# A hybrid attention and delta-rule layer on one core: weights laid out by partition, the second half of x normed among the shift and scale's quarters, the values' turns one projection later

## The chip, the cores and the metric

The program runs on one core of a Trainium2 chip. The core has a matrix engine (TensorE, PE in the profile; its weight loads are PEld), VectorE (DVE), ScalarE (ACT), GpSimd (POOL) and SyncE (SP, which here only issues DMAs), and 16 DMA engines that move data between memory and the core. The metric is the device time of one execution in microseconds (us); the time of a kernel is the median of its runs.

## The reference, cut to what matters

The layer takes 1024 latent tokens and 256 context tokens of width 1024, modulates them by a shift and a scale that a small matrix product makes from a vector c (and c_ctx for the context), projects them with one matrix w_in of 4112 columns, and mixes them by neighbourhood attention and by a gated delta rule in both directions.

```
shift, scale, gate = jnp.split(jax.nn.silu(c) @ w_ada + b_ada, 3, axis=-1)
h = rmsnorm(x, g_pre) * (1.0 + scale[:, None]) + shift[:, None]
hc = rmsnorm(xc, g_pre) * (1.0 + scale_c) + shift_c
na_q, na_k, na_v, na_z, g_qkv, g_z, g_b, g_a = jnp.split(h @ w_in, IN_SPLITS, axis=-1)
...
o_na = neighborhood_attention(heads(na_q), heads(na_k), heads(na_v),
                              heads(na_kc), heads(na_vc), rpb)
q, k, v = gdn_qkv(g_qkv, conv_w)
...
o_g, o_gc = bidirectional_gdn(q, k, v, g, beta, qc, kc, vc, gc, betac)
y = jnp.concatenate([o_na * jax.nn.silu(na_z), o_g * jax.nn.silu(g_z)], axis=-1) @ w_out
x = x + gate[:, None] * rmsnorm(y, g_post)
```

## The kernel before

Matrix products run in 32-bit form as three products of high and low parts: every weight and every activation is split into hi (a copy in the matrix engine's own 32-bit type) and lo (the rest), and a product is hi·hi + lo·hi + hi·lo. So each group of products is three lines of the code: L446, L450, L451 where channels come out as partitions, and L459, L460, L461 where tokens do. The activations after the norm are the tiles hh and hl (128 partitions by 8 blocks of 128 channels by 1024 tokens), chh and chl for the context.

The first stage is `phase0`. It loads the first half of x (512 tokens, tiles x), turns it so that channels lie in the partitions (tile raw) and takes its sums of squares on ACT. A helper, `norms` (L216), makes a row of factors from such sums: an addition on DVE (L148), a power on POOL (L149), a spread on DVE (rr, L221), a turn on PE (prr, L224), a copy on ACT (rba for the first half, rbb for the second, L225). The shift and scale come in four quarters, each of 256 channels, by `ada(q)` (L266): four loads of w_ada into the tile wada (7 buffers), a matmul for each block of 128 rows into par (L276), a copy of par by DVE (rows, L288), four small matmuls that put the result into partitions (pa, L292), two short DVE operations (ab, am), and `modulate` (L235) for the quarter's two blocks of channels: a scaling on DVE (L238), the high part on ACT (L244), the low part on DVE or POOL (L245, L242). Then `products(q)` (L305) takes the two blocks into six sums that stay open over all quarters: values for four tiles of tokens (pv) and query and key (pq, pk).

Behind the quarters come the loads of a gate's weights (wg), the second half of x (tiles xta and xtb of 4 blocks by 256 tokens, `load_t`), its squares on ACT (xsa, xsb, L330) and their sums over channels by matmuls against a column of ones (pss, L335, one output column each), `norms`, the gate's projection (pz, L446 to L451 out of wgh and wgl), `mod(0)` and `mod(1)` for the second half, the second half's values and query and key, and the context (xtc).

The order on an engine is set by the code's order and by a scheduler that moves an instruction forward where its inputs are early. Loads of the first stage are chained on SP's queue by `chain` (L205), in the order of the code. A load waits for its buffer: x and the squares xs share a tag with 4 buffers, wada is shared by wg, xta and xtb.

`load_w` (L414) loads a piece of w_in, copies it on ACT into the high part and subtracts on POOL (L432) for the low part. In `phase2` the delta rule's inputs are projected, convolved (acc, L798 to L800, on DVE) and turned, head by head, by the steps of a string (L755): R the gate of the residual, V the values' convolution, p a projection of `projections`, T and B the turns of query and key, U the turns of the values (vtp on PE, L737; vs on ACT, L739, whose buffer is shared with the tile rot of T). Between the steps DVE solves small triangular systems (tb and vb, L989 and L992). One of the projections is that of the first 264 value channels (wl_nv, pv), whose weights are split in four pieces.

## Time and profile before

| | us |
|---|---|
| runs | 914.02, 919.75, 919.37 |
| median | 919.37 |
| the profiled execution | 925.77 |
| span of its core | 924.1 |
| PE busy | 865.4 (94%) |
| DVE busy | 534.1 (58%) |
| ACT busy | 418.3 (45%) |
| POOL busy | 371.2 (40%) |

The span is the time from the core's first to its last instruction in the profile. A row of a timeline reads: start, duration, engine, line of the code and operation, output and inputs, partitions by elements, count; in brackets how long the engine stood idle before it and what released it. A row of the table by stretches gives for each engine the busy time and the number of instructions, then the clock that was granted to PE (1.00 is full speed), the busy share of the DMA engines and the rate that they moved. A matmul of fp32 inputs stands in the trace as two rows, so that four matmuls of pa are 8 there, and 8 of pss are 16.

### The profile page before, as it was taken

What the parts mean: (1) busy time and instruction counts of PE and PEld (TensorE: products, weight loads), DVE (VectorE), ACT (ScalarE), POOL (GpSimd) and SP (SyncE); (2) the same over time, 40 slices, a digit from 0 to 9 for tenths busy, and PEclk for the clock granted to TensorE, in tenths of its full rate; (3) what the DMA queues carried; (4) which work ended last, traced back from release to release, by engine and by line L of the source; (5) the groups of instructions that cost most, each with busy time, mean ns of one, the idle gap of its engine ahead of it and who ended that gap; (6) DMA issues with size and microseconds to landing.
All of it is one profiled execution on the core that took longest, in us unless ns stands there. A gap on an engine that the chain in (4) does not pass through costs nothing.

```text
span 924.1 us, 16864 instructions
## 1 busy us (share of the span) xinstructions
PE 865.4 (94%) x6178; PEld 724.0 (78%) x6178; DVE 534.1 (58%) x1191; ACT 418.3 (45%) x1171; POOL 371.2 (40%) x435
## 2 busy tenths in 40 slices
PE   5998999999999998998997999899999997999997
PEld 3687988788788776778976878688888886788785
DVE  3416326535644699779437723477777775673442
ACT  4235323554654643651434534455556546553211
POOL 1313122263463461455231311566757558632110
PEclk9977999999999999999997999899999999799999
DMA  9853351254544723842899775999839324223261
GB/s 309 261 165 109 122 172 49 79 166 162 147 146 153 212 92 126 264 108 70 252 250 251 224 218 175 397 263 227 301 79 304 132 70 149 80 73 134 71 207 65
DMA packets 126441, 157.85 MB, mean 171 GB/s; under 512 B 29893, under 2 KB 99862, under 8 KB 124182
## 3 DMA queue, kind: packets, MB, share of 16 engines
q1 hardware_dynamic: 98870, 142.58, 49.8%
q10 hardware_dynamic: 27488, 14.19, 6.0%
q8 instruction: 49, 0.80, 0.4%
q14 instruction: 34, 0.28, 0.1%
HBM read 107.67 MB, written 52.42 MB: 173 GB/s over the span
## 4 chain that ended last, share of the span: by engine, by line
PE 69%; DMA 12%; DVE 12%; ACT 3%; issue 2%; SPq 1%; POOL 0%; ACTq 0%; DVEq 0%; POOLq 0%
PE py L1204 3%; PE py L1206 3%; PE py L1205 3%; PE pz L446 3%; PE pz L450 3%; PE pz L451 3%; PE pl L674 2%; PE pv L459 2%; PE po L701 2%; PE pv L460 2%; PE pl L683 2%; PE pv L461 2%; PE po L696 2%; DVE tb L989 2%; PE pc L670 2%
## 5 line engine op out<-in xcount | busy, mean ns | idle before, releaser
L662 POOL TENSOR_TENSOR gm<-gt,mk 128x288 f32<-128x288 f32 (+1 forms) x64 | 64.2, 1009 | 26.5 <-DVE nm L679 22.4
L1111 POOL TENSOR_SCALAR kd<-kt,kd 128x128 f32<-128x128 f32 x72 | 43.1, 603 | 35.7 <-PE pa L1130 35.1
L680 ACT ACTIVATE pt<-pt,nm 128x288 f32<-128x288 f32 (+1 forms) x64 | 36.8, 575 | 41.7 <-DVE nm L679 41.1
L446 PE MATMUL pz<-hh,wh_gz 128*128 128x512 f32 x112 | 46.3, 413 | 1.0 <-DVE sl_k L509 1.0
L450 PE MATMUL pz<-hl,wh_gz 128*128 128x512 f32 x112 | 45.7, 408 | 0.0
L451 PE MATMUL pz<-hh,wl_gz 128*128 128x512 f32 x112 | 45.3, 405 | 0.0
L678 DVE TENSOR_REDUCE mi<-pc 128x1 f32<-128x256 f32 x64 | 26.9, 421 | 30.1 <-PE pc L670 29.6
L460 PE MATMUL pv<-wh_nv,hl 128*128 128x264 f32 x128 | 39.7, 316 | 4.2 <-DVE hl L245 4.2
L459 PE MATMUL pv<-wh_nv,hh 128*128 128x264 f32 x128 | 38.3, 318 | 5.0 <-DVE st_z L534 3.6
L685 DVE COPY tl<-pl 96x384 f32<-96x384 f32 (+1 forms) x64 | 35.3, 552 | 11.0 <-PE pl L683 10.4
L679 DVE CUSTOM_DVE_ANT_0 pt<-pl,gm,mi 128x288 f32<-128x288 f32 (+1 forms) x64 | 36.0, 563 | 8.2 <-PE pl L674 4.6
L683 PE MATMUL pl<-c,pt 128*96 128x128 f32 (+1 forms) x192 | 34.3, 289 | 5.4 <-ACT pt L680 5.3
L461 PE MATMUL pv<-wl_nv,hh 128*128 128x264 f32 x128 | 39.0, 311 | 0.4 <-POOL wl_nv L432 0.4
L931 ACT ACTIVATE em<-em,gc 128x128 f32<-128x128 f32 x80 | 25.5, 390 | 30.5 <-DMA em<-gc_dram 26.0
L946 DVE SCALAR_TENSOR_TENSOR pm<-pk,beta,em 128x128 f32<-128x128 f32 x80 | 23.6, 344 | 24.6 <-PE pk L939 14.3
L989 DVE TENSOR_TENSOR tb<-ab,vb 120x31 f32<-120x31 f32 (+15 forms) x62 | 32.3, 521 | 7.7 <-DMA ab<-ab_dram 6.0
L950 POOL TENSOR_SCALAR_AFFINE_SELECT qe<-qe 128x256 f32<-128x256 f32 x32 | 26.9, 841 | 21.1 <-DVE qe L949 21.0
L460 PEld LDWEIGHTS pv<-wh_nv,hl 128*128 128x128 f32 x128 | 27.1, 213 | 8.8 <-DVE hl L245 4.5
L1114 POOL TENSOR_SCALAR vb<-v,beta 128x128 f32<-128x128 f32 x40 | 24.2, 605 | 24.1 <-DVE y L1120 16.3
L432 POOL TENSOR_TENSOR wl_gq<-wr_gq,wh_gq 128x512 fp32r<-128x512 f32 x8 | 15.1, 1899 | 44.8 <-ACT wh_gq L431 27.4
L459 PEld LDWEIGHTS pv<-wh_nv,hh 128*128 128x128 f32 x128 | 26.5, 216 | 8.1 <-DVE st_z L534 3.8
L1130 PE MATMUL pa<-vn,kd 128*128 128x128 f32 x144 | 28.8, 286 | 4.2 <-ACT vn L1128 3.1
(440 smaller groups left out, 2924.3 us busy)
## 6 DMA issues: line engine op xcount, KB each, us to landing
wada<-in_w_ada SPq DMA_DIRECT2D x32, 256.0 KB, 5.5
em<-gc_dram SPq DMA_DIRECT2D x20, 256.0 KB, 4.1
pm_dram<-pm SPq DMA_DIRECT2D x20, 256.0 KB, 2.8
pmf<-pm_dram SPq DMA_DIRECT2D x8, 640.0 KB, 7.2
tm_dram<-tm SPq DMA_DIRECT2D x8, 640.0 KB, 4.3
kk<-qk_dram SPq DMA_DIRECT2D x16, 320.0 KB, 8.6
tm<-tm_dram SPq DMA_DIRECT2D x4, 1280.0 KB, 9.7
kq_dram<-kq SPq DMA_DIRECT2D x4, 1152.0 KB
```

The source lines that it names most:

```text
L446: r = nc.tensor.matmul(ps, wh, xh, start=(k == 0), stop=False)
L450: nc.tensor.matmul(ps, wh, xl, start=False, stop=False)
L451: nc.tensor.matmul(ps, wl, xh, start=False, stop=(k == KC - 1))
L459: nc.tensor.matmul(ps, xh, wh, start=(k == 0), stop=False)
L460: nc.tensor.matmul(ps, xl, wh, start=False, stop=False)
L461: nc.tensor.matmul(ps, xh, wl, start=False, stop=(k == KC - 1))
L662: nc.gpsimd.tensor_tensor(gm[:, :n].rearrange("p (n c r) -> p n c r", c=nco, r=4), gv, mk[:, mo:mo + n].rearrange("p (n c r) -> p n c r", ...
L679: nc.vector.tensor_tensor_reduce(pt[:, :n], pl[:, :n], gm[:, :n], -1.0, mi, ALU.add, ALU.min, nm)
L680: nc.scalar.activation(pt[:, :n], pt[:, :n], AF.Exp, bias=nm, scale=-1.0, accum_out=sums[:, ct, hh, 0:1])
L683: nc.tensor.transpose(pl[:m, rc * P:(rc + 1) * P], pt[:, rc * m:(rc + 1) * m], self.ident)
L989: nc.vector.tensor_tensor(t3, bc(ab[:, 0:m, m:m + 1], [r, m, n]), bc(vb[:, m:m + 1, m:], [r, m, n]), ALU.mult)
L1111: nc.gpsimd.tensor_scalar(kd, kt_[:, t, :], self.kd[:, h, d, t:t + 1], None, ALU.mult)
```

## The change

It has four parts.

1. The host lays the weights out by partition. The shift and scale part of w_ada becomes an array of quarters in which a partition's rows follow each other, so one DMA brings a wada tile (4 KB a partition), where two brought it in pieces of 1 KB. The gate part becomes an array of its own. w_in becomes one flat array in which each piece that `load_w` loads lies in one run a partition (W_PARTS, W_OFF), so that the two-part pieces are one DMA too.
2. The second half of x is loaded behind the first quarter's weights, in four tiles of two blocks by 512 tokens (tag x). Its squares and their sums are taken with the second quarter, `norms` follows, and its blocks are modulated at a width of 512 among the third and fourth quarters. The squares, and rr of the norm, share the one buffer sq. The context's squares and sums are later, behind the products of the fourth quarter, and its modulation is ahead of the rest of the gate's projection.
3. In `load_w`, where the weights come in four pieces (halves=4), the subtract of the second and fourth piece runs on DVE.
4. In the string of steps the values' turns U stand behind the last projection p instead of ahead of it.

```diff
-        "xt": f("x").reshape(S, D)[512:].reshape(2, 256, 8, P).transpose(0, 3, 2, 1),
+        "xt": f("x").reshape(S, D)[512:].reshape(512, 8, P).transpose(2, 1, 0),
...
-                    for n in range(2):
-                        c0 = 1024 * n + 256 * q
-                        chain(wa[:, :, n, :], I["w_ada"][P * k2:P * k2 + 256, c0:c0 + 256].rearrange(
-                            "(k p) n -> p k n", p=P))
+                    chain(wa, I["w_ada"][q][:, k2:k2 + 2])
...
+            def load_t(src, nm, pool_tag, bufs, kk):
+                r = []
+                for k in range(0, KC, kk):
+                    w = p0.tile([P, kk, D // kk], F32, name=f"xt{nm}{k}", tag=pool_tag, bufs=bufs)
+                    chain(w, src[:, k:k + kk, :])
+                    r.extend(w[:, j, :] for j in range(kk))
+                return r
+
+            def squares(xr, nm, pss, kk):
+                n = D // kk
+                for k in range(0, KC, kk):
+                    s_ = p0.tile([P, kk, n], F32, name=f"xs{nm}{k}", tag="sq", bufs=1)
+                    for j in range(kk):
+                        nc.scalar.activation(s_[:, j, :], xr[k + j], AF.Square)
+                    for j in range(kk):
+                        for i in range(n // P):
+
+                            nc.tensor.matmul(pss[:, i:i + 1], s_[:, j, P * i:P * i + P], self.ones, start=(k + j + i == 0),
+                                             stop=(k + j == KC - 1 and i == n // P - 1))
+
+            def second(ks):
+                for k in ks:
+                    modulate(xr[k], self.hh[:, k, 512:], self.hl[:, k, 512:], k, 0, rb2)
+
+            ada(0)
+            xr = load_t(I["xt"], "a", "x", 4, 2)
+            ada(1)
+            products(0)
+            pss = at("pss", "tb", 2)
+            squares(xr, "a", pss, 2)
+            rb2 = rbt("b")
+            norms(g1, rb2, pss[:, 0:4], nc.vector)
+            ada(2)
+            products(1)
+            second(range(4))
+            ada(3)
...
+            xc = load_t(I["cxt"], "c", "wada", 7, 4)
+            products(2)
+            second((4, 5))
             products(3)
+            second((6, 7))
...
-            mod(0)
             next(gates)
...
+            src = self.I["w_in"]
+            (load or nc.scalar.dma_start)(raw.rearrange("p k n -> p (k n)"), bass.AP(
+                src.tensor, W_OFF[tuple(c0) if isinstance(c0, list) else ((c0, n),)] + k0 * n, [[KC * n, P], [1, kk * n]]))
             nc.scalar.copy(hi, raw)
-            nc.gpsimd.tensor_tensor(lo, raw, hi.bitcast(F32), ALU.subtract)
+            (nc.vector if halves > 2 and k0 % 4 else nc.gpsimd).tensor_tensor(lo, raw, hi.bitcast(F32), ALU.subtract)
...
-                for c in "RVppTpUpB":
+                for c in "RVppTppUB":
```

In the rows below a name ends in a number that tells buffers of the same kind apart, and the shape is that of one instruction. On PE, before, the fourth quarter's pa is followed by the third quarter's last products, the sums of squares of the second half stand behind these, and the fourth quarter's products behind the sums:

```order
L292 MATMUL pa_475<-c_60,rows_473 128x2 x4
L446 MATMUL pq_0_208<-hh,wqk_h 128x512
L450 MATMUL pq_0_208<-hl,wqk_h 128x512
L451 MATMUL pq_0_208<-hh,wqk_l 128x512
L446 MATMUL pq_0_208<-hh,wqk_h 128x512
L450 MATMUL pq_0_208<-hl,wqk_h 128x512
L451 MATMUL pq_0_208<-hh,wqk_l 128x512
L335 MATMUL pss<-ones,xsa_538 128x1 x4
L335 MATMUL pss<-ones,xsa_542 128x1 x4
```

On PE, now, behind the second quarter's products (the first two pieces of the squares, xsa_352 and xsa_363, were summed ahead of and among them):

```order
L467 MATMUL pk_0_209<-hl,wqk_h 128x512
L468 MATMUL pk_0_209<-hh,wqk_l 128x512
L347 MATMUL pss<-ones,xsa_374 128x1 x8
L347 MATMUL pss<-ones,xsa_385 128x1 x8
L242 MATMUL prr_402<-c_60,rr_400 128x128 x4
L291 MATMUL par_408<-wada_409,sc 32x512 x2
L291 MATMUL par_408<-wada_413,sc 32x512 x2
L291 MATMUL par_408<-wada_417,sc 32x512 x2
L291 MATMUL par_408<-wada_421,sc 32x512 x2
L307 MATMUL pa_437<-c_60,rows_435 128x2 x4
L291 MATMUL par_501<-wada_502,sc 32x512 x2
```

The norm of the second half (prr), the third quarter's par and its pa now follow the sums directly, with no products between them, and the fourth quarter's par stands in one piece.

On DVE, before, two quarters follow each other, each with its copy of rows, ab, am, two scalings and two low parts:

```order
L288 COPY rows_388<-par_355 128x512
L245 SCALAR_TENSOR_TENSOR hl<-raw,ab_310,hh 128x512 x2
L296 TENSOR_TENSOR ab_395<-pa_390,cols 128x8
L297 SCALAR_TENSOR_TENSOR am<-ab_395,cols 128x4
L238 SCALAR_TENSOR_TENSOR raw<-raw,am,rba 128x512 x2
L245 SCALAR_TENSOR_TENSOR hl<-raw,ab_395,hh 128x512 x2
L288 COPY rows_473<-par_440 128x512
```

On DVE, now, from the norm of the second half to the third quarter's low parts:

```order
L166 TENSOR_SCALAR rq_y_x_397<-pss 128x4
L239 TENSOR_SCALAR rr_400<-rq_y_x_397 128x512
L256 SCALAR_TENSOR_TENSOR xta_264<-xta_264,am,rbb 128x512 x2
L256 SCALAR_TENSOR_TENSOR xta_266<-xta_266,am,rbb 128x512 x2
L263 SCALAR_TENSOR_TENSOR hl<-xta_264,ab_255,hh 128x512
L263 SCALAR_TENSOR_TENSOR hl<-xta_266,ab_306,hh 128x512
L303 COPY rows_435<-par_408 128x512
L311 TENSOR_TENSOR ab_442<-pa_437,cols 128x8
L312 SCALAR_TENSOR_TENSOR am<-ab_442,cols 128x4
L256 SCALAR_TENSOR_TENSOR raw<-raw,am,rba 128x512 x2
L256 SCALAR_TENSOR_TENSOR xta_268<-xta_268,am,rbb 128x512 x2
L263 SCALAR_TENSOR_TENSOR hl<-raw,ab_442,hh 128x512 x2
```

Four scalings and two low parts of the second half stand ahead of the copy of the third quarter's rows, and two more scalings ahead of that quarter's own low parts.

On DVE in phase 2, before, behind the triangular solve's operations tb and vb, at the gate projection st_z that stands next to the first value channels' products:

```order
L989 TENSOR_TENSOR tb_3553<-ab_3550,vb_3552 120x207
L992 TENSOR_TENSOR vb_3552<-vb_3552,tb_3553 120x23x9
L989 TENSOR_TENSOR tb_3553<-ab_3550,vb_3552 120x220
L992 TENSOR_TENSOR vb_3552<-vb_3552,tb_3553 120x22x10
L534 SCALAR_TENSOR_TENSOR st_z_3866<-st_z_3866,pz_1_3841 128x512
```

and now:

```order
L449 TENSOR_TENSOR wl_nv_6_3854<-wr_nv_6_3852,wh_nv_6_3853 128x528
L1006 TENSOR_TENSOR tb_3511<-ab_3508,vb_3510 120x207
L551 SCALAR_TENSOR_TENSOR st_z_3824<-st_z_3824,pz_1_3799 128x512
L1009 TENSOR_TENSOR vb_3510<-vb_3510,tb_3511 120x23x9
L1006 TENSOR_TENSOR tb_3511<-ab_3508,vb_3510 120x220
```

The subtract of the fourth weight piece is on DVE, and st_z stands three operations of the solve earlier.

More of the change, by code (lines that the diff above doesn't have):

```diff
@@ L87, with by_partition @@
 MTOT = _o
+W_PARTS = ([((1288, 248), (4096, 16)), ((0, P), (512, P)), ((1024, 264),)]
+           + [((c, P),) for c in [1536] + [P * j + o for j in range(1, 4) for o in (0, 512, 1536)]
+              + [2048 + P * j for j in range(12)] + [3584 + P * j for j in range(4)]])
+W_OFF = {}
+_o = 0
+for _w in W_PARTS:
+    W_OFF[_w] = _o
+    _o += D * sum(_n for _, _n in _w)
+def by_partition(w):
+    return w.reshape(KC, P, -1).transpose(1, 0, 2)
 def layout_inputs(inp):
@@ L349, in phase0 @@
                 self.qk_out(0, i, 0, pqk[i])
-            def mod(j):
-                for k in range(KC):
-                    sl = slice(512 + 256 * j, 768 + 256 * j)
-                    modulate(xr[j][k], self.hh[:, k, sl], self.hl[:, k, sl], k, 0, rbs[j])
-            mod(0)
             next(gates)
             pss = at("pssc", "tb", 2)
-            xr.append(load_t(I["cxt"], "c", pss[:, 0:2]))
-            for j in range(2):
-                g = g1[2 * j:2 * j + 2]
-                if j == 0:
-                    mod(1)
-                    norms([0, 1], rbs[2], pss[:, 0:2], nc.vector)
-                self.values(vp, wv, 1, g)
+            squares(xc, "c", pss, 4)
+            rbc = rbt("c")[:, :256]
+            norms([0, 1], rbc, pss[:, 0:2], nc.vector)
+            self.values(vp, wv, 1, g1)
             for i in range(2):
@@ L394, in res_gate @@
             nc.sync.dma_start(wt.rearrange("p (k n) -> p k n", k=2),
[L395 removed]
+                              I["w_adg"][q][:, k:k + 2, :])
             wts.extend(wt[:, 256 * j:256 * j + 256] for j in range(2))
```

41 lines of the change are left out of this document (6 added, 35 removed).

## The prediction

> **What bounds the kernel now.** I read the table of engine times by stretch first, with the granted clock beside it, because the change touches one early stage and one place at 330 to 425 us.
>
> ```profile
> core 0: us, PE busy (x) PEld busy (x) DVE busy (x) ACT busy (x) POOL busy (x), PEclk, DMA share, GB/s
> 0.00:25.00 25.00, 15.72 (x73) 9.29 (x75) 8.74 (x16) 11.13 (x19) 4.37 (x11) 0.91 0.99 309
> ...
> 60.00:80.00 20.00, 20.00 (x86) 18.20 (x86) 3.88 (x12) 4.26 (x10) 1.02 (x1) 0.63 0.26 80
> 80.00:95.00 15.00, 10.75 (x66) 10.26 (x64) 12.54 (x23) 10.19 (x26) 6.93 (x8) 0.77 0.41 125
> 130.00:230.00 100.00, 100.00 (x524) 83.55 (x523) 50.87 (x75) 45.10 (x109) 35.60 (x45) 1.00 0.39 120
> 230.00:330.00 100.00, 100.00 (x521) 81.45 (x520) 59.44 (x90) 54.94 (x136) 44.21 (x44) 1.00 0.53 159
> 330.00:430.00 100.00, 88.46 (x469) 73.23 (x468) 87.77 (x150) 49.89 (x145) 54.21 (x46) 0.97 0.47 143
> ```
>
> TensorE (PE) is full at full clock from 130 us on, so whatever the first 95 us gain or lose reaches the end one for one until 330 us, where VectorE (DVE) is nearly as busy as PE. The first 25 us hang on the DMA engines (share 0.99), 60 to 80 us on a PE that is always busy but granted 0.63 of its clock, 80 to 95 us on DVE. Then I read PE's timeline of this stage, row by row.
>
> ```profile
> 54.23 1.05 PE L335 MATMUL pss<-ones,xsa 128*128 128x1 f32 x8 [0.38 <-ACT xsa L330]
> 55.64 3.25 PE L335 MATMUL pss<-ones,xsa 128*128 128x1 f32 x24 [0.36 <-ACT xsa L330]
> ...
> 62.39 1.70 PE L335 MATMUL pss<-ones,xsb 128*128 128x1 f32 x8
> ...
> 64.54 5.11 PE L335 MATMUL pss<-ones,xsb 128*128 128x1 f32 x24
> ...
> 74.42 0.63 PE L451 MATMUL pk<-hh,wqk_l 128*128 128x512 f32 x1
> 74.84 0.46 PE L446 MATMUL pk<-hh,wqk_h 128*128 128x512 f32 x1
> 75.14 0.39 PE L450 MATMUL pk<-hl,wqk_h 128*128 128x512 f32 x1
> 75.37 0.40 PE L451 MATMUL pk<-hh,wqk_l 128*128 128x512 f32 x1
> ...
> 87.12 0.59 PE L460 MATMUL pv<-wh_nv,hl 128*128 128x264 f32 x1 [4.25 <-DVE hl L245]
> ...
> 91.91 0.35 PE L460 MATMUL pv<-wh_nv,hl 128*128 128x264 f32 x1
> ...
> 94.06 2.73 PE L335 MATMUL pssc<-ones,xsc 128*128 128x1 f32 x24
> ```
>
> From 54.23 to 58.89 us PE runs nothing but sums of squares with one output column. From there a 512-column matmul starts every 0.42 us (74.42 to 74.84) until 75.1 us, when it is every 0.23 us (75.14 to 75.37): the clock is at half, though PE's row is full. The second slow stretch, 87.12 to 91.91, follows a wait of 4.25 us for the low parts hl of the second half. The 2.73 us of one-column sums at 94.06 had no slow work behind them, so the limit lies between 2.7 and about 4.3 us of low activity.
>
> **What the change takes away.** Four terms, all in the first stage.
>
> The first quarter of the shift and scale weights (256 KB x 8, 2.1 MB) comes in pieces of 4 KB a partition. The nearest rows are the loads of x, which have that shape, against these weights as now.
>
> ```profile
> 5.00:10.00 5.00, 3.70 (x18) 3.71 (x19) 0.76 (x2) 3.63 (x7) 0.00 (x0) 1.00 1.02 404
> 10.00:15.00 5.00, 4.54 (x30) 2.48 (x30) 2.50 (x4) 2.79 (x6) 1.28 (x2) 1.00 1.10 352
> ```
>
> At 352 GB/s 2.1 MB take 6.0 us, at 404 5.2: R1 = 0.8, ends 0 and 1.3. I take 0.8, since PE waits for these loads there. Later quarters are hidden under PE's own work.
>
> R2, the half clock of 58.9 to 75.1. The sums of 6.81 us would take 4.30 as at 54 to 59 us: 2.5 saved. The other 9.4 us are products, which save 45% (0.42 to 0.23): 4.3. Together 6.8, if the sums no longer stand in one block; their work itself stays.
>
> R3, the wait of 4.25 and the half clock behind it (4.8 us of work, 2.3 saved): 6.6. The second half is then modulated some 30 us before its values are due.
>
> R4, the two waits of PE for squares, 0.38 and 0.36: 0.7. **Removed: 14.9 us.**
>
> **What it adds.** The sums now stand in three pieces: 8 matmuls ahead of the second quarter's products, 8 within them, 16 behind them; then comes the norm, and PE has nothing else in front of it. These rows carry the prices.
>
> ```profile
> 69.69 0.16 DVE L148 TENSOR_SCALAR rq_y_x<-pss 128x4 f32<-128x4 f32 x1 [4.56 <-PE pss L335]
> ...
> 71.05 0.43 DVE L221 TENSOR_SCALAR rr<-rq_y_x 128x512 f32<-128x512 f32 x1 [0.36 <-POOL rq_y_x L149]
> ```
> ```profile
> 33.84 0.95 PE L292 MATMUL pa<-c,rows 128*128 128x2 f32 x8
> 34.72 1.93 PE L276 MATMUL par<-wada,sc 128*32 128x512 f32 x16
> ```
> ```profile
> 36.73 0.69 DVE L288 COPY rows<-par 128x512 f32<-128x512 f32 x1
> 37.34 2.53 DVE L245 SCALAR_TENSOR_TENSOR hl<-raw,ab,hh 128x512 fp32r<-128x512 f32 x2
> ...
> 42.63 1.42 DVE L245 SCALAR_TENSOR_TENSOR hl<-raw,ab,hh 128x512 fp32r<-128x512 f32 x2
> ...
> 52.74 1.41 DVE L238 SCALAR_TENSOR_TENSOR raw<-raw,am,rba 128x512 f32<-128x512 f32 x2
> ```
> ```profile
> 37.99 1.33 POOL L432 TENSOR_TENSOR wl_nv<-wr_nv,wh_nv 128x528 fp32r<-128x528 f32 x1 [9.64 <-DMA wada<-in_w_ada]
> ```
> ```profile
> 53.12 1.06 ACT L330 ACTIVATE xsa<-xta 128x1024 f32<-128x1024 f32 x1 [3.92 <-DMA xta<-in_xt]
> ...
> 78.10 0.59 ACT L225 COPY rbb<-prr 128x512 f32<-128x512 f32 x1 [1.64 <-PE prr L224]
> ```
>
> - A1, squares. One buffer of squares now serves all four pieces, so the last square cannot start until PE has read the one before: a wait of one square less its overlap, 0.8 of 1.06 (ends 0 and 1.1).
> - A2, the norm's round trip, pss to DVE to GpSimd (POOL) to DVE to PE: 69.65 to 71.48 in the rows, and a start: 2.0. Before, products covered it; now PE stands (ends 1.8 and 2.2).
> - A3. DVE's copy of the third quarter's rows is now queued behind the second half: rbb 0.59 on ScalarE (ACT), then four scalings (0.705 each, 2.8), two hl (1.4) and the copy (0.69) make 5.5, while PE has only the third quarter's par, 1.93. Idle 3.6 (ends 2.2, if the two hl slip behind, and 4.3).
> - A4. Behind pa two more scalings (1.4) stand ahead of the hl that the third quarter's products need: 0.33 + 1.41 + 1.41 + 0.7 = 3.9 after pa, against par 1.93 and four or five products of about 1: wait 1.0 (ends 0 and 2.1).
> - A5. The pair hl at 37.34 took 2.53 beside a POOL subtract (37.99), the pair at 42.63 took 1.42 with POOL idle: 1.1 lost. POOL has six such pieces in the new stretch (two hl, four splits of weights), where DVE is now what PE waits for. Two of six on the path: 2.0 (ends 0 and 7.8).
> - A6. These 8 to 10 us hold two waits and little dense work, so the clock drops; price as behind the 4.25 us wait: 2.3 (ends 0 and 9: two quarters' products, 11.2 us, at 0.42 in place of 0.23 a matmul).
> - A7. At the second quarter the wait A1, pa (0.95) and 8 sums (16 rows of the trace, 2.15) make 3.9 us of low activity, between the 2.7 that held and the 4.7 that fell: 60% of 2.0 = 1.2 (ends 0 and 2.3).
> - A8. The fourth quarter's par comes in one row with its weights long there: 1.93 in place of 3.2 in three pieces: -1.2.
>
> **Added: 0.8 + 2.0 + 3.6 + 1.0 + 2.0 + 2.3 + 1.2 - 1.2 = 11.7.** Net of the stage -3.2.
>
> At nothing I cost the load of the second half ahead of the second quarter's weights. Its cover is this row: the second quarter's last weights were in by 25 us, and pa of that quarter ran at 33.84.
>
> ```profile
> 25.07 0.63 ACT L431 CAST wh_nv<-wr_nv 128x528 fp32r<-128x528 f32 x1 [2.19 <-DMA wr_nv<-in_w_in]
> ```
>
> 2.1 MB at 350 GB/s shift that to 31 us, so 2.9 us of cover stay; without it the stage would lose up to 6 - R1. The layout of the other weights is at nothing too: they load under a full PE (130 to 230 us). [...]
>
> **Phase 2.** Two edits; these rows hold their prices.
>
> ```profile
> 332.74 0.87 PE L737 MATMUL vtp<-c,acc_v 128*128 128x128 f32 x6 [1.66 <-DVE acc_v L800]
> ...
> 354.67 0.97 PE L737 MATMUL vtp<-c,acc_v 128*128 128x128 f32 x4 [4.15 <-ACT vs L739]
> ```
> ```profile
> 423.18 0.59 PE L459 MATMUL pv<-wh_nv,hh 128*128 128x264 f32 x1 [3.59 <-DVE st_z L534]
> ```
> ```profile
> 419.92 1.35 DVE L989 TENSOR_TENSOR tb<-ab,vb 120x207 f32<-120x207 f32 x1
> 421.30 0.38 DVE L992 TENSOR_TENSOR vb<-vb,tb 120x207 f32<-120x207 f32 x1
> 421.71 0.39 DVE L989 TENSOR_TENSOR tb<-ab,vb 120x220 f32<-120x220 f32 x1
> 422.14 0.39 DVE L992 TENSOR_TENSOR vb<-vb,tb 120x220 f32<-120x220 f32 x1
> 422.44 0.68 DVE L534 SCALAR_TENSOR_TENSOR st_z<-st_z,pz 128x512 f32<-128x512 f32 x1
> ```
>
> The values' turns one projection later take the 1.66 away, but the 4.15 that follows ends when DVE has let go of a buffer that vs shares, and DVE does not get there sooner: what PE gains first it waits later. 0 (ends -1.7 and +0.8, one pair of tb and vb). The two subtracts of wl_nv move from POOL to DVE: +0.7 each, less the 0.96 by which a DVE operation such as the tb at 419.92 (1.35 against 0.39) stood longer beside POOL's. And st_z now stands three operations (1.16) earlier. For st_z: +0.7 - 0.96 - 1.16 = -1.4; I take **-1.5** with the first subtract's balance (ends +1.4 and -5, the whole wait and the half clock behind it).
>
> **Sum.** -14.9 + 11.7 - 1.5 = -4.7. The profiled execution took 925.77, so 921.1 there; it is 0.7% above the median of 919.37, and on the median the sum is **914.7**.
>
> **Rivals.**
> - The clock holds and DVE keeps up: A4, A5, A6 and A7 are 0. For it: 2.73 us of sums at 94.06 did no harm. Against it: A2 and A3 are in the order of the queues and leave 5.6 us. 914.7 - 6.5 = 908.2.
> - The two sides of the split collide: every one of POOL's six pieces (1.3 each) holds a DVE operation that PE waits for, A5 = 7.8. For it 37.34; against it 42.63, where DVE went free between POOL's pieces. 914.7 + 5.8 = 920.5, no gain. [...]
> - The slower side: the clock stays at half from the norm's wait through the third and fourth quarters' products, as it did for 16 us after the sums of 54 to 59. A quarter's products are 24 of 0.12 and 12 of 0.23, 5.6 us; two quarters, the 24 gate matmuls behind them (5.5) and two tiles of values (24 of 0.12 each, 5.8) are 22.5 us of work, each us of which costs 0.83 more (0.42 for 0.23): 18.7, in place of A6 and A7 (3.5). 914.7 + 15.2 = 929.9, slower. It decides only if it lasts into the values, 21 us of work; against it speaks the recovery at 92 us, after 4.8.
> [...]
>
> **How the numbers follow.** The forecast as summed (911 to 918 by the ends of A3, A5 and A6) has 0.50, the first rival 0.24, the collision 0.14, the slow clock 0.06; 0.06 is for what I have not seen. A measurement of this kernel tells about 1% from no change: below 910.2 is faster, above 928.6 slower. Faster: the first rival and the forecast's tail, 0.27; slower 0.07; the rest, 0.66, no change that can be told. The range goes to 905 (first rival with R1 and phase 2 at their better ends) and 922 (collision with A3 at its worse end).
>
> **What the next profile would show.** R2: no granted 0.5 beside a full PE at 60 to 75 us. R3: no wait of PE on hl above 2 us at the second half's values. A2, A3: two PE waits near 45 to 55 us, of about 2 us (prr on rr) and 3 to 4 us (pa on rows). A5: pairs of hl above 2 us beside POOL. Phase 2: the wait on st_z under 2.5 us, the wait on vs still above 4. I am wrong if the second half's squares are late (pss waits of several us), or if the second quarter's par waits for its loads.

## The result, and the profile after

| | before | after |
|---|---|---|
| median of 20 runs, us | 919.0 | 923.25 |
| lowest and highest, us | 914.02, 923.06 | 919.59, 927.96 |
| the profiled execution, us | 925.77 | 927.96 |
| its span, us | 924.1 | 926.2 |
| PE busy, us | 865.4 | 858.4 |
| PE idle (span less busy), us | 58.7 | 67.8 |

The changed kernel takes 1.0057 of the time before [1.0039, 1.0075], 4.25 us more. One run of 1630.52 us was disturbed and is left out of the ratio and of the highest time, as is one run each of two kernels below. The forecast was 914.7 in a range of 905 to 922: the time is outside the range, and the sum had the wrong sign. PE was busy for 7 us less, as a gain would have it, and idle for 9 us more.

The table by stretches of the changed kernel, to be laid beside the first one of the prediction:

```profile
core 0: us, PE busy (x) PEld busy (x) DVE busy (x) ACT busy (x) POOL busy (x), PEclk, DMA share, GB/s
0.00:25.00 25.00, 14.17 (x74) 10.72 (x75) 8.86 (x16) 12.23 (x21) 4.81 (x11) 0.92 0.93 348
25.00:60.00 35.00, 29.36 (x172) 21.64 (x171) 9.11 (x16) 11.40 (x19) 8.06 (x7) 0.79 0.48 176
60.00:80.00 20.00, 18.07 (x103) 13.88 (x103) 14.47 (x19) 11.35 (x22) 9.56 (x7) 0.78 0.64 228
80.00:95.00 15.00, 15.00 (x97) 13.63 (x96) 6.31 (x17) 6.07 (x16) 2.18 (x3) 1.00 0.38 122
...
330.00:430.00 100.00, 86.27 (x450) 72.22 (x449) 85.95 (x148) 47.88 (x143) 50.49 (x44) 0.93 0.47 144
```

The trouble of 60 to 95 us is gone: PE is full at 80 to 95 us, where it stood for 4.25 us. It has come back earlier: between 25 and 60 us PE is idle for 5.6 us (0.9 before) at a clock of 0.79 (0.94 before). And from 330 to 430 us PE is idle for 13.7 us where it was 11.5, at 0.93 where it was 0.97.

PE's timeline of the changed kernel shows where the first stage stands:

```profile
17.39 1.02 PE L307 MATMUL pa<-c,rows 128*128 128x2 f32 x8 [0.89 <-DVE rows L303]
...
21.76 1.25 PE L476 MATMUL pv<-wh_nv,hh 128*128 128x264 f32 x4 [3.35 <-ACT hh L262]
...
35.15 1.93 PE L347 MATMUL pss<-ones,xsa 128*128 128x1 f32 x16
...
49.03 1.95 PE L347 MATMUL pss<-ones,xsa 128*128 128x1 f32 x16 [0.77 <-ACT xsa L343]
...
52.94 1.08 PE L242 MATMUL prr<-c,rr 128*128 128x128 f32 x4 [1.97 <-DVE rr L239]
53.96 3.64 PE L291 MATMUL par<-wada,sc 128*32 128x512 f32 x16
59.50 1.83 PE L307 MATMUL pa<-c,rows 128*128 128x2 f32 x8 [1.90 <-DVE rows L303]
61.26 3.64 PE L291 MATMUL par<-wada,sc 128*32 128x512 f32 x16
...
67.94 0.39 PE L477 MATMUL pv<-wh_nv,hl 128*128 128x264 f32 x1 [1.81 <-DVE hl L263]
```

The four waits in brackets behind 49 us are A1 (0.77), A2 (1.97), A3 (1.90) and A4 (1.81). The two rows of par took 3.64 us, where the prediction's row has 1.93 for the same 16: the clock was at half. The granted clock of the same execution in pieces of 5 us says for how long (the columns are those of the table above):

```profile
50.00:55.00 5.00, 3.03 (x21) 1.98 (x24) 0.91 (x3) 0.58 (x1) 1.02 (x1) 0.66 0.02 3
55.00:60.00 5.00, 3.10 (x19) 0.74 (x9) 4.35 (x7) 3.80 (x6) 1.90 (x2) 0.50 0.55 186
60.00:65.00 5.00, 4.90 (x23) 1.83 (x22) 3.56 (x4) 2.59 (x4) 4.99 (x4) 0.50 0.51 175
65.00:70.00 5.00, 3.17 (x17) 2.85 (x18) 5.00 (x6) 4.07 (x9) 2.15 (x2) 0.84 0.98 338
```

The timelines of DVE and then of POOL, same execution, show what A5 is made of:

```profile
58.66 0.69 DVE L303 COPY rows<-par 128x512 f32<-128x512 f32 x1
61.37 0.17 DVE L311 TENSOR_TENSOR ab<-pa,cols 128x8 f32<-128x8 f32 x1 [2.02 <-PE pa L307]
61.57 0.87 DVE L312 SCALAR_TENSOR_TENSOR am<-ab,cols 128x4 f32<-128x4 f32 x1
62.48 3.42 DVE L256 SCALAR_TENSOR_TENSOR raw<-raw,am,rba 128x512 f32<-128x512 f32 x2
...
67.14 2.45 DVE L263 SCALAR_TENSOR_TENSOR hl<-raw,ab,hh 128x512 fp32r<-128x512 f32 x2
```
```profile
58.10 3.00 POOL L260 TENSOR_TENSOR hl<-xta,hh 128x512 fp32r<-128x512 f32 x2 [5.76 <-ACT hh L259]
61.11 1.31 POOL L449 TENSOR_TENSOR wl_nv<-wr_nv,wh_nv 128x528 fp32r<-128x528 f32 x1
62.38 1.29 POOL L449 TENSOR_TENSOR wqk_l<-wr_qk,wqk_h 128x512 fp32r<-128x512 f32 x1
63.61 1.74 POOL L449 TENSOR_TENSOR wgl<-wr_gz,wgh 128x512 fp32r<-128x512 f32 x1
```

POOL works without a gap from 58.1 to 65.4 us. The pair raw takes 3.42 where two took 1.41, the pair hl 2.45 for 1.41, and am 0.87, until POOL's piece is done (62.44 and 62.42 us), though ab, twice as wide, took 0.17 just before.

In phase 2, PE's two long waits of the changed kernel, and DVE's timeline ahead of the second:

```profile
355.21 1.12 PE L754 MATMUL vtp<-c,acc_v 128*128 128x128 f32 x4 [5.79 <-ACT vs L756]
...
421.23 0.59 PE L478 MATMUL pv<-wl_nv,hh 128*128 128x264 f32 x1 [4.54 <-DVE wl_nv L449]
```
```profile
418.86 1.30 DVE L1006 TENSOR_TENSOR tb<-ab,vb 120x192 f32<-120x192 f32 x1
420.20 0.36 DVE L1009 TENSOR_TENSOR vb<-vb,tb 120x192 f32<-120x192 f32 x1
420.48 0.70 DVE L449 TENSOR_TENSOR wl_nv<-wr_nv,wh_nv 128x528 fp32r<-128x528 f32 x1
421.10 0.37 DVE L1006 TENSOR_TENSOR tb<-ab,vb 120x207 f32<-120x207 f32 x1
421.38 0.68 DVE L551 SCALAR_TENSOR_TENSOR st_z<-st_z,pz 128x512 f32<-128x512 f32 x1
```

The waits of 1.66 and 4.15 us before the values' turns have become one of 5.79, and the wait of 3.59 on st_z has become one of 4.54 on the moved subtract itself.

Two marks help to place the loss. The first matmul of gpl_q, which ends the first stage, starts at 129.13 us before and at 127.57 now; the last turn of values (vtp) starts at 441.7 before and 442.7 now. So in these two executions the stage gained 1.6 us and phase 2 lost 2.5; behind 440 us another 1.1 was lost. That this reading is itself deceptive, the experiments show.

### The profile page after: what moved, and what is told of

It is laid out like the page before. It is cut to its first block, busy times and chain, and to the rows that moved or that the text cites. A ratio compares the mean times of both kernels' runs of the same rounds, so it can differ in the third digit from the quotient of the medians.

```text
span 926.2 us, 16805 instructions
## 1 busy us (share of the span) xinstructions
PE 858.4 (93%) x6178; PEld 722.6 (78%) x6178; DVE 530.2 (57%) x1181; ACT 417.9 (45%) x1169; POOL 368.1 (40%) x429
## 4 chain that ended last, share of the span: by engine, by line
PE 71%; DVE 10%; DMA 10%; ACT 3%; issue 2%; SPq 1%; POOL 1%; DVEq 0%; POOLq 0%; ACTq 0%
PE py L1221 3%; PE py L1223 3%; PE py L1222 3%; PE pz L468 3%; PE pz L463 3%; PE pz L467 3%; PE pl L691 2%; PE pv L477 2%; PE pv L476 2%; PE pv L478 2%; PE po L718 2%; PE pc L687 2%; PE pl L700 2%; PE pa L1141 2%; PE gpl_k L468 2%
## 5 line engine op out<-in xcount | busy, mean ns | idle before, releaser
L700 PE MATMUL pl<-c,pt 128*96 128x128 f32 (+1 forms) x192 | 32.3, 277 | 5.4 <-ACT pt L697 5.3
L449 POOL TENSOR_TENSOR wl_gq<-wr_gq,wh_gq 128x512 fp32r<-128x512 f32 x8 | 15.7, 1966 | 52.1 <-ACT wh_gq L448 27.4
L1006 DVE TENSOR_TENSOR tb<-ab,vb 120x31 f32<-120x31 f32 (+15 forms) x62 | 30.1, 486 | 6.8 <-DMA ab<-ab_dram 5.1
L815 DVE SCALAR_TENSOR_TENSOR acc_v<-xp_v,cols,acc_v 128x1282 f32<-128x1282 f32 x16 | 26.2, 1639 | 11.7 <-ACT acc_v L813 11.5
L707 ACT COPY tcx<-pc 128x256 f32<-128x256 f32 x64 | 23.6, 369 | 18.2 <-PE pc L705 18.0
```

The lines of the kernel that those rows point to most:

```text
L700: nc.tensor.transpose(pl[:m, rc * P:(rc + 1) * P], pt[:, rc * m:(rc + 1) * m], self.ident)
```

## The experiments

Theory: the stage's gain is as summed or smaller, and phase 2 gives it back. Rivals: the stage gained nothing and the first profile was an unlucky execution of the old stage; or what is lost lies behind 440 us, where the change moves no work but the scheduler orders it anew. A ratio is to the kernel before, run side by side with the kernel in question; brackets hold its 95% interval.

### The parts one by one

The stage alone (e1 in later texts): the changed kernel with both edits of phase 2 undone.

```diff
-            (nc.vector if halves > 2 and k0 % 4 else nc.gpsimd).tensor_tensor(lo, raw, hi.bitcast(F32), ALU.subtract)
+            nc.gpsimd.tensor_tensor(lo, raw, hi.bitcast(F32), ALU.subtract)
...
-                for c in "RVppTppUB":
+                for c in "RVppTpUpB":
```

> The changed kernel with the subtract back on GpSimd and the values' turns back ahead of the last projection: only the first stage and the weights' layout are new. Theory 1 (the stage is worth what the two traces show at 130 us, -1.6 us, and the two edits of phase 2 lose 4 to 6): 917.5 us, PE's wait on st_z near 420 us back at about 3.6 us. Theory 2 (DVE is the bound from 330 to 360 us, so what the stage gains is waited for there): 919 us, and a wait on vs near 355 us longer than 4.15 by what the stage gained. Theory 3 (the loss lies in the late order, at 665 us, whichever part is changed): 922 us or more.

Phase 2 alone: the kernel before with these two edits made.

> The kernel before with only the two edits of phase 2 (subtract of two pieces on DVE, values' turns behind the last projection); the weights load as before. Theory 1: 922 to 925 us, with a wait of about 4.5 us on the DVE subtract near 423 us. Theory 2: 919 to 921 us. Theory 3: 922 us or more, with a wait on qe or y near 665 us.

The changed kernel with the subtract alone back on POOL (e3 in later texts), and the changed kernel with the old string alone:

> The changed kernel with the subtract of all four pieces back on GpSimd. Theory 1, if the subtract is the costlier of the two edits: 919 to 920 us, the wait of 4.54 us on wl_nv gone and one of about 3.6 on st_z in its place. If the values' turns are: 922 to 923 us. Theory 3: 923 us with the waits near 665 us, or any time if the late order falls otherwise.

> The changed kernel with the values' turns back ahead of the last projection. Theory 1, if the subtract is the costlier edit: 922 to 923 us, the wait on wl_nv still 4 to 5 us, the one wait of 5.79 on vs split again into two of 1.7 and 4.2 (their sum the same). If the values' turns are: 919 to 920 us.

| | median | ratio |
|---|---|---|
| the whole change | 923.25 | 1.0057 [1.0039, 1.0075] |
| stage alone | 930.39 | 1.0117 [1.0077, 1.0158] |
| phase 2 alone | 925.51 | 1.0057 [1.0028, 1.0086] |
| without the subtract on DVE | 920.74 | 0.9995 [0.9968, 1.0023] |
| without the later turns | 922.43 | 1.0035 [1.0001, 1.0069] |

These are misses for every theory that adds: the parts cost 10.2 and 5.3 us over the 920.17 of the kernel before beside them, together 15.6, and both at once 4.25. The waits do follow the edits. PE's waits from 330 to 430 us (in all, how often, the longest), without the subtract on DVE and then without the later turns:

```profile
PE vtp L754 <- ACT vs L756: 4.7, 1, 4.7
PE pv L476 <- DVE st_z L551: 4.1, 1, 4.1
PE tp L837 <- ACT sq L843: 3.8, 3, 2.4
```
```profile
PE pv L478 <- DVE wl_nv L449: 5.0, 1, 5.0
PE vtp L754 <- ACT vs L756: 3.0, 1, 3.0
PE vtp L754 <- DVE acc_v L817: 1.9, 1, 1.9
PE tp L837 <- ACT sq L843: 1.5, 2, 0.9
```

With the subtract on POOL the wait is on st_z again; with the old string the turns wait twice again, for 4.9 together. So the subtract moves a wait and lengthens it, and the later turns join two waits in one. They also lengthen a third: the turns of query and key (tp) wait for their squares (sq) on ACT for 2.6 to 4.6 us in the four profiled kernels with the later turns, and for 1.3 to 1.6 in the seven without. But 10 us for the stage alone stands in no wait of the first 440 us: its two marks are 127.1 and 440.9, ahead of the profiled execution before. So both ends had to be tried by themselves.

### The first stage by itself

The first stage alone, what lies behind it left out and hh written out by one DMA:

```diff
-                    self.phase2()
-                    self.pf = fx.enter_context(tc.tile_pool(name="pf", bufs=1, side="right", reuse_waits="tile"))
-                    self.phase_a2()
-                with tc.tile_pool(name="g3", bufs=1, side="left", reuse_waits="tile") as self.g3:
-                    self.phase_b()
+                        self.nc.sync.dma_start(self.out.rearrange("(a p) n -> p a n", p=P), self.hh.bitcast(F32))
```

It was made of the kernel before, of the changed one, of the one before with the new weight layout, and of the changed one with the old layout.

> The first stage of the kernel before alone: everything behind it is left out, and one DMA writes the high parts of the modulated activations to the output. It takes some 130 to 140 us; what counts is its distance to the next three. Theory 1 (the stage itself became faster as the sum says): the changed stage is 1.5 to 3.2 us shorter. Theory 2 (the half clock of 59 to 75 us was one draw among several, since the same stage in the run with only phase 2 changed ended 5 us earlier than in the first profile): runs of this kernel scatter by 4 us or more, and the changed stage is not shorter in the median, or longer.

> The first stage of the changed kernel alone, cut and written out in the same way. Theory 1: 1.5 to 3.2 us below the stage of before. Theory 2: within 1 us of it, or above, with a scatter as large.

> The first stage of before with only the weights laid out by partition. Theory 1: R1 alone, 0.8 us below the stage of before (0 to 1.3). Rival: the layout is what the whole gain of the stage comes from, 1.5 us or more.

> The changed first stage with the weights loaded as before. Theory 1: 0.8 us above the changed stage, so 1 to 2.4 below that of before. Theory 2: the early second half costs by itself as much as it saves: within 1 us of the stage of before, or above it.

They took 132.87, 138.6, 131.75 and 137.78 us. On the old stage the layout is worth 1.1 (0.8 if a run of 555 us among the six is left out), near R1's 0.8; on the changed one it cost 0.8. Both are within the scatter of the runs. Of the 5.7 us between the stages 2.8 are an artefact: in the cut of the changed stage the output DMA stood among the stage's own stores, and PE waited 2.8 us on st_z, which it does not in the whole kernel. So both were cut again with that DMA ordered behind the last store:

> The first stage of before alone once more, with the one DMA that writes the output put behind the last store of the stage, so that nothing of the stage waits for it (in the cuts of the second call it stood among the stage's stores, and in the changed stage PE then waited 2.8 us on st_z for a buffer). Some 20 us longer than the cut of before. Theory 1 (the changed stage is the faster one): 1.5 to 3.2 us more than the next run. Theory 2: not more than 1 us apart.

> The first stage of the changed kernel alone, with the output written behind the stage's last store. Theory 1: 1.5 to 3.2 us below the run before this. Theory 2: within 1 us of it, or above.

143.33 and 144.2 us: the changed stage costs 0.9 by medians, a miss for theory 1. The runs tell more than the medians. The old stage took 143.33 to 144.44 in four runs and 139.65 and 139.97 in two; in the first cut it was 132.53 to 133.33 in three and 128.74 and 129.23 in two. The changed stage took 143.75 to 144.66 each time. So the old stage has a lucky draw, 4 us shorter, which the changed one did not show. By means the changed stage costs 1.8, and against the two short runs alone 4.4.

What is drawn is the place of the half clock. Two executions with the same instructions up to 120 us, the kernel before as profiled and then the second of the two kernels cut at 470 us that are told of below, which has the old stage:

```profile
60.00:65.00 5.00, 5.00 (x23) 4.81 (x23) 0.05 (x1) 0.61 (x2) 0.00 (x0) 0.50 0.00 0
65.00:70.00 5.00, 5.00 (x24) 5.00 (x25) 0.29 (x2) 0.00 (x0) 0.01 (x1) 0.50 0.11 25
70.00:75.00 5.00, 5.00 (x18) 4.32 (x17) 0.96 (x5) 1.70 (x4) 1.02 (x1) 0.50 0.32 75
```
```profile
60.00:65.00 5.00, 5.00 (x39) 5.00 (x39) 0.34 (x2) 0.73 (x2) 0.49 (x1) 0.84 0.12 29
65.00:70.00 5.00, 5.00 (x22) 4.31 (x21) 1.57 (x5) 1.93 (x4) 0.52 (x1) 0.77 0.35 81
70.00:75.00 5.00, 5.00 (x25) 4.12 (x25) 3.46 (x8) 2.84 (x7) 0.57 (x1) 1.00 0.56 209
```

In the second, the clock was at 0.84, 0.77 and 1.00 where the first had 0.50 throughout, and gpl_q started at 122.1 in place of 129.1, 7 us earlier. Six profiled executions with the old stage's order (one of them with the new layout, one with four matmuls more, both told of below) ended it at 122.1 to 129.1; the mean is 125.2 and the one that the prediction was made from is the last of them. The changed stage ended at 127.1 to 129.9 in five, mean 128.3. The traces hold the granted clock with its times, so what PE did up to the start of gpl_q can be added up:

| up to the start of gpl_q, us | it starts | PE idle | PE busy at half clock | the start less the idle time and half of the busy time at half clock |
|---|---|---|---|---|
| the execution of the prediction | 129.1 | 14.4 | 27.5 | 101.0 |
| old stage, six executions | 122.1 to 129.1, mean 125.2 | 12.4 to 14.4, mean 13.2 | 15.7 to 27.8, mean 22.1 | 100.1 to 102.0 |
| changed stage, five executions | 127.1 to 129.9, mean 128.3 | 18.4 to 19.9, mean 19.4 | 19.5 to 27.0, mean 22.8 | 97.2 to 97.6 |

The last column is an estimate of the time that the stage would take at full clock without a wait (a matmul of 512 columns starts every 0.42 us at half clock and every 0.23 at full). It hardly moves within a stage while the starts differ by 7 us, so the scatter of the old stage is the clock's and, by 2 us at most, that of PE's waits. The table also says what the change did: the work became about 3 us shorter, the time at half clock did not shrink, and PE is idle for 6.2 us more.

The mend that the rows suggest (e13 in later texts): let PE do the third quarter's par (1.93 us at full clock) while the norm makes its round trip.

```diff
-            norms(g1, rb2, pss[:, 0:4], nc.vector)
             ada(2)
+            norms(g1, rb2, pss[:, 0:4], nc.vector, self.par_last)
```

(with `norms` ordering its first turn on PE behind par_last, the last matmul of par).

> The changed first stage alone, output written behind its last store, with one order added: the norm of the second half (prr) comes on PE behind the third quarter's par, which moves that quarter's rows, pa and products ahead of the norm. It tests A2, A3 and A6, the norm's round trip, the copy of rows queued behind the second half, and the half clock behind both. If these are where the stage loses what it gained: 136 to 140 us against 144.2 of the changed stage and 143.3 of the stage before. If the waits only move elsewhere: 143 to 145 us.

141.39 us, 2.8 less than the changed stage in the same cut. From 25 to 60 us, the changed stage and then the mended one:

```profile
25.00:60.00 35.00, 29.37 (x184) 21.11 (x187) 9.82 (x19) 12.26 (x21) 9.33 (x8) 0.84 0.51 190
```
```profile
25.00:60.00 35.00, 34.04 (x215) 24.70 (x214) 9.07 (x18) 12.06 (x23) 11.21 (x9) 0.90 0.59 213
```

PE is busy for 34.0 of 35 us in place of 29.4, at 0.90 in place of 0.84: the idle time and the low clock of A2 and A3 were the greater part of what the changed stage lost.

### Up to 470 us

Both kernels' phase 2 with the old stage, cut behind phase 2, without and with the two edits:

> The kernel before up to the end of phase 2; the merging, the attention, the scan and the output projection are left out, and the output is written by one DMA behind the last stores. Its distance to the next run is the price of the two edits of phase 2 without the order of what comes later.

> The same cut with both edits of phase 2, the subtract of two pieces on DVE and the later turns of the values. My prediction's -1.5 us would be seen as 1.5 less than the run before this. Theory 1 as the traces show it now: 2.5 to 4.2 us more. Rival (the loss lies behind phase 2, in the order of scan and attention): the same within 1 us.

473.57 (471.7 to 473.8) and 471.78 (464.7 to 477.0). This settles nothing: the second scatters by 12 us, and the cut takes away the work that PE has to fill in behind 423 us (from there to 470 us PE is busy for 9.9 us in the first cut and for 46.8 in the whole kernel).

### What stands behind 440 us

The weight layout alone, on the kernel before (part 1 of the change, nothing else; e14 in later texts):

> The kernel before with only the weights laid out by partition. Alone in the first stage it measured 1.1 us less than before. Theory A (parts add up): 918 to 919 us. Theory B (any edit that shifts the scheduler's clock reorders attention, scan and output behind 440 us, and that order is worth several us either way): a distance from 918.5 of 3 us or more is possible, and it is then found in the stretches behind 440 us and not ahead of them.

915.32 us, 0.9949 [0.9916, 0.9982]: the one clear gain. Its profiled execution, 920.95, is the longest of its ten, so the profile does not show where the gain lies. Then a kernel whose edit should cost next to nothing, four matmuls that nothing reads, 0.9 us of PE's time, behind the first stage's last query and key:

```diff
             self.qk_out(0, 1, 2, pk)
+            nul = at("nul", "ta", 3)
+            for i in range(4):
+                nc.tensor.matmul(nul, wqk[1][0][0], self.hh[:, 0, 0:512], start=(i == 0), stop=(i == 3))
```

> The kernel before with four matmuls of 512 columns more at the end of the first stage, whose result nothing reads: 0.9 us of work on PE. Theory A: 919 to 921 us. Theory B: outside of 917 to 923 us, with the difference in the stretches behind 440 us.

931.87 us, 1.0102 [1.0067, 1.0137]: 11.8 us for 0.9 us of work. Its stage ended at 123.0 in the profile, which is one of its three short executions (925.06). In phase 2 PE's instructions come in the order of the kernel before, but for one; behind it the scheduler has put attention, the scan and the out-projection into another order. How it arrives at one is not shown here.

The mended stage in the whole kernel, with the subtract on POOL and the later turns kept:

> The whole changed kernel with the order of e13 added and the subtract of all four pieces on GpSimd; it is e3 but for the order in the first stage. If the order is worth what e13 is to show, and nothing shifts behind 440 us: 4 to 6 us below e3's 920.7, so 914 to 917 us, faster than before by half a per cent. Theory B: anywhere from 910 to 925, with the first stage's part of it as in e13.

925.05 us, 1.0054 [1.0027, 1.0082], though its stage ended at 122.8 in the profile (a short execution, 919.53), 4.8 before the changed kernel's. It has the same kind of order at the end as the stage alone and the four matmuls: from the last reciprocal of attention's sums (rs) to the last row but one of the scan's turned outputs (ot) these three take 47.7 us, the other eight whole kernels (before, after and two that are told of below among them) about 41.

From the first matmul of the out-projection to the end it is 109.2 to 110.4 us in these three and 100.5 to 100.6 in the other eight. Laid side by side behind the last turn of the values, PE's instructions of the stage alone and of the four matmuls differ in the place of 36 out of some 3930. Those of the changed kernel and of the first three others with edits of phase 2 differ from those of the layout alone in the place of 33 to 70, and from those of the stage alone in 585 or more. So the slow end explains why the parts did not add up, and it is not what the changed kernel lost by.

So the order was held fixed. The stage alone again (e17 in later texts), with each engine's instructions from phase 2 on put into the order that they have in the kernel with the layout alone, by order edges without waits:

```diff
+    ins = tc.nc.cur_bb.bb.instructions
+    for seq in json.loads(zlib.decompress(base64.b85decode(LATE))).values():
+        n, last = k.mark, None
+        for d in seq:
+            n += d
+            if last is not None:
+                tc.add_manual_dep(ins[n], ins[last].name, mybir.DependencyInfo(mybir.DependencyClass.NoSync,
+                                  mybir.DependencyReason.DATA), reason="late order")
+            last = n
```

> e1 (the new first stage and layout, phase 2 as before; 930.4 us) with each engine's order from phase 2 on set to the one that e14 (915.3 us) has. The work is that of e1, only its order behind 440 us differs. If the order is what e1 lost by (theory B): e14's time plus the first stage's 0.9 to 1.5, 915 to 918 us. If the stage's transfers, clock or buffers reach into the later phases by another way: 925 to 931 us.

920.58 us, 1.0026 [1.0007, 1.0044], against 930.39, 1.0117 [1.0077, 1.0158] for the same instructions: the order is worth 9.8 us by medians and 8.4 by the two ratios. It is the order behind 440 us, since in phase 2 both have the same on PE but for one instruction. The scan's last product on PE, first as the scheduler ordered it, then with the order fixed:

```profile
854.38 0.39 PE L1156 MATMUL pos<-vn,qe 128*128 128x128 f32 x2
```
```profile
840.12 0.39 PE L1156 MATMUL pos<-vn,qe 128*128 128x128 f32 x2
```

When the out-projection's matmuls begin on PE (at 819.8 and 817.7 us), the scan has seven such products still to go in the first and four in the second, and among those matmuls one comes only every 3 to 6 us. So the scan ends 14 us later, and the last of its turned outputs (ot) start at 864.3 in place of 854.8.

At last the mended stage with the same fixed order:

> The new stage with the third quarter's par ahead of the norm (e13, 2.8 us below the changed stage), layout by partition, phase 2 as before, and the order from phase 2 on as in e14. Theory B: 2.8 us below e17, 912 to 915 us, the shortest of all and below the kernel before by about 6 us. If the mended stage's gain is waited for later: equal to e17.

915.73 us, 0.9982 [0.9953, 1.0011]: 4.9 less than the changed stage with that order beside it, and 3 below the kernel before where some 6 were expected.

## Why the prediction was wrong

**R2, the half clock of 58.9 to 75.1, is the first step that failed.** The change did not take the half clock away, it moved it: up to gpl_q PE worked for 22.8 us at half clock in the mean of the changed stage, for 22.1 in the mean of the old one. By the sum it should have fallen by some 11 us: R2's 6.8 and R3's 2.3 less the 3.5 of A6 and A7 are 5.6 us saved, and work at half clock takes about twice its time (0.42 us for 0.23 a matmul of 512 columns). R2 was also counted in full from one execution, the worst of the six seen since. In their mean the old stage ends 4.0 us earlier than there, so more than half of R2 was never to be had in the median. The sum against the execution's own time, laid on the median, carried the bad draw over as if every run had it. The two tables of one stage, at 0.50 and at 0.84, 0.77 and 1.00, show the draw; what decides it is not shown. The limit of 2.7 to about 4.3 us of low activity, by which the terms on the clock were priced, was the author's estimate from one execution; no run tests it. The 7 us between the two executions of these tables are 0.8% of 919, more than the whole sum.

**A5, A6 and A8: sizes.** A5 cost DVE 3.7 in place of 2.0 (raw 2.0, hl 1.0, am 0.7); PE waited only 1.81 for it and A4 together, since par at half clock took up the rest. A6 was put at 2.3 and stands at half clock from about 53 to 65 us: the two rows of par (1.7 each over 1.93) and pa (0.9 over 0.95) alone are 4.3. A8 came out the other way: its one piece of par costs 3.64 and not 1.93, which is one of the two rows just counted. **A7** came as summed: the second quarter's products of 38.2 to 41.3 us ran at half clock (0.50), about 1.4 us over (1.2). Not every DVE operation beside POOL took longer: the copy of rows at 58.66 took 0.69, as it did before with POOL idle (36.73), while the pairs raw and hl took 3.42 and 2.45 where 1.41 is their time alone, and am 0.87 in place of 0.16.

**A1 to A4: right or near.** The square was 0.77 late (0.8). The norm's round trip cost 1.97 (2.0). From the start of par to pa it took 5.54 us, the 5.5 of A3's chain; PE stood for only 1.90 of it, since par at half clock filled the rest. A4 was 1.81 in place of 1.0. **R3 and R4**: the wait of 4.25 is gone, no wait on hl is above 1.81, and no other wait on squares is left.

**The rivals.** Of the collision, 3.7 of 7.8 came on DVE. The clock did not stay low into the values: it is 1.00 from 80 to 95 us. None of them is what made the time.

**R1 was right at its place and half lost behind it.** pa of the first quarter starts at 17.39 in place of 18.26 in the trace before, 0.87 earlier, and the transfers of 10 to 15 us ran at 402 GB/s where it was 352. But on ACT the first squares of the second half now stand ahead of hh, as its timeline shows, and the first product starts at 21.76 in place of 22.27, 0.5 earlier:

```profile
19.95 1.15 ACT L343 ACTIVATE xsa<-xta 128x512 f32<-128x512 f32 x2 [0.86 <-DMA xta<-in_xt]
21.00 1.32 ACT L262 ACTIVATE hh<-raw,ab 128x512 fp32r<-128x512 f32 x2
```

The load of the second half was costed at nothing; its squares on ACT, which every moved step brings along, were not costed at all.

**The stage's net, -3.2, came out as a loss.** By itself +0.9 (means +1.8); by the start of gpl_q in whole kernels +3.1 (128.3 against a mean of 125.2). Against the layout alone, with the late order the same, the stage is at 1.0026 and 0.9949: 0.8%, 7 us by the ratios of two series of runs and 5.3 by medians. The first cuts with the layout in both, 138.6 and 131.75, are 6.9 apart, 2.8 of it the artefact. The mend gives 2.8 back in the cut and 4.9 in the whole, so most of the loss is PE's empty time between the sums and the third quarter's products: behind 25 us and up to gpl_q PE is idle for 3.8 us in the mended stage, for 7.6 to 9.5 in the changed one and for 3.9 to 5.1 in the old one. A2 to A4 were near in size, but the sum set R2 against them, and R2 did not come.

**Phase 2, -1.5, was +2.5 in the profiles.** Of the values' turns, two waits became one, 5.81 to 5.79 (4.7, 4.7 and 3.4 in three other kernels), as summed; the wait of tp on sq, which grew by 1.0 to 3.3, was not priced at all. The subtract was wrong in its consumer. The prediction weighed what its 0.7 us does to st_z; it did not ask who waits for the subtract itself. That is the value product, and the subtract stands on DVE behind solve operations of 1.3 us, while on POOL it was all but ready in time (a wait of 0.4 before). PE's wait at that place grew from 3.6 to 5.0 with the subtract alone and from 4.1 to 4.5 beside the later turns.

From the start of gpl_q to the last turn of the values it took 312.6 to 314.5 us in the six profiled kernels without the two edits, 315.2 with the subtract alone, 315.8 and 318.0 with the turns alone, 315.1 and 316.8 with both. So each seems to cost; which costs more is not settled, as the clock in that stretch differs too (0.93 to 0.97 behind 330 us). With the subtract back on POOL the whole change is at 0.9995 [0.9968, 1.0023], but the 318.0 is its phase 2: what it gained lies behind that (473.5 us in place of 483.5 in the profiles, with nearly the same order), and the cause of that is open.

**"Whatever the first 95 us gain or lose reaches the end one for one" holds to 440 us.** In the six kernels without phase 2's edits the stage ends within 6.1 us and the last turn of the values within 5.4. But the work behind is put in order by a scheduler that answers to any edit ahead: 0.9 us of matmuls cost 11.8, and order alone gave 9.8 back. Such a term belonged into the range, in both signs, some 10 us wide. It was luck that the changed kernel did not pay it.

**What made the 4.25 us.** The layout alone, the stage with the layout and the fixed order, and the whole change have nearly the same late order; they stand at 0.9949, 1.0026 and 1.0057. So the layout with its order is -0.5%, the stage +0.8% and the two edits of phase 2 +0.3%, by ratios of three series; the intervals of the last two, [1.0007, 1.0044] and [1.0039, 1.0075], overlap a little.

What is open: the share of each edit of phase 2; and how much of the 4.7 us that the layout alone gains is transfers (some 1 in the stage) and how much order, since behind phase 2 its order differs from that of the kernel before in 255 places. That kernel, 0.9949 [0.9916, 0.9982], is the version that beats both; the mended stage with its order, 915.73, is equal to it within the scatter.

## What to carry to other kernels

A term that rests on the granted clock is priced from several executions, never from one, and it is asked where the low clock goes when the work ahead of it is moved. Where a scheduler orders the code, an edit is judged with the rest of the order held fixed, or its own effect drowns in what it stirs up hundreds of microseconds later. And an operation that moves to another engine is priced twice: for those queued behind it, and for those who wait for its own result.

## What the runs showed of the hardware that was not expected

The same stage runs for quite different times at half clock in different executions: up to gpl_q PE was busy at half clock for 15.7 to 27.8 us in six, and it got there up to 7 us earlier or later (0.50, 0.50, 0.50 against 0.84, 0.77, 1.00 in three stretches). In the profiled execution before, the clock stayed at half, up to there, for 6.8, 17.1 and 6.8 us at a time, and in the changed kernel's for 6.8, 3.4, 13.7 and 3.4, multiples of the shortest. And a very small DVE operation took longer beside POOL than a large one alone: am, 128x4, took 0.87 us and ended with POOL's piece (62.44 and 62.42 us), right behind ab, 128x8, with 0.17; with POOL idle, at 73.66 us, am took 0.16 and the scalings of 128x512 behind it 1.41 the pair.
